# Layer 0's first gate: its sums moved from matmuls to weighed sums, and its product with the heads moved to the fourth head

## The chip, the cores and the metric

The kernel runs on one core of a Trainium2 chip. The time is the device time of one execution in microseconds (us). The core has five engines that run side by side, each through its own list of instructions: TensorE (PE, matrix products), VectorE (DVE), ScalarE (ACT), GpSimd (POOL), and SyncE (SP), which issues most of the transfers from HBM. On-chip data lies in SBUF (128 partitions); PE writes its results into PSUM, eight banks of 128x512 fp32.

## The reference

A transformer of two layers on 256 latent tokens `x` and 256 context tokens `ctx`, width 1024, in fp32. Each layer makes six vectors from a condition (`c` for the latents, `c_ctx` for the context), and uses them as shift, scale and gate around a mixer and an MLP:

```python
mod = (silu_c @ ada_w[i] + ada_b[i])[:, None, :]
mod_c = silu_cc @ ada_w[i] + ada_b[i]
sh1, sc1, g1, sh2, sc2, g2 = jnp.split(mod, 6, axis=-1)
h = x * (1.0 + sc1) + sh1
y, yc = retention_mixer(h, hc, ...)          # layer 0; layer 1: neighbourhood_mixer
x = layer_norm(DN_ALPHA * x + g1 * y, ln_g[i, 0], ln_b[i, 0])
h = x * (1.0 + sc2) + sh2
x = layer_norm(DN_ALPHA * x + g2 * sq_relu_mlp(h, mlp_w1[i], mlp_w2[i]), ln_g[i, 1], ln_b[i, 1])
```

In layer 0 the context takes the same way with `sh1c`, `g1c` and so on. The retention mixer has four heads; the result of each, `o`, is normalized, multiplied by `silu(gate projection)`, and goes through its 512 rows of `w_o`; `y` is the sum over the four heads. So `g1 * y` is a product of a vector over the 1024 columns with the sum of four heads' outputs.

## The kernel before

**Numbers and weights.** Each fp32 product is made of three matmuls (`mm3`) on parts: a high part, cast to a shorter format, and a low part, the difference. Weights come in units of 128x1024 (512 KB). A unit is loaded on SP's queue into a raw slot (`fetch`, L255; the pool `rawp` has four slots), ACT casts it (`hi`), DVE subtracts (`lo`), and PE uses both. `hi` and `lo` have five buffers each, so that up to five units are prepared ahead (`take`, L282). A raw slot is free again when `lo` is made.

**The order.** Each helper records every operation through one line, L84, so all rows carry that line, and one goes by the names of the tiles. A scheduler fixes each engine's order when the kernel is built; places where `dve.on` or `act.on` is set keep the order of the code. On the chip each engine goes through its list in order, and an instruction that waits holds up all behind it on its engine, also on the queues of SP and POOL.

**Tiles.** The residual `R` has four tiles of 128 tokens by 1024: 0 and 1 (latents) lie in one buffer, `R_104`, and 2 and 3 (context) in another, `R_105`. At first they hold x and ctx.

**The heads** (`for h in range(RH)`, L1045). The first head's q and v are made in a prologue. Then for each head: `pq` (q, then k, two units each), rotation by position (`rotate`, L1003: ACT casts, DVE products and sums), `pv` (four units) and its evacuation into `vh` by ACT and `vl` by DVE, the scores `pS` (24 matmuls) masked by DVE, the gate projections `pg` of tiles 0 and 1, `po` (scores by v), the other two gate projections, a transposition, and the output products `pw` of the head's 512 rows of `w_o`. The first head has the order `pg` (tile 0), `pS`, `pg` (tile 1), `po`. For each `pw` piece of 128x512, `accumulate` (L756) multiplies by the gate `G` on DVE and adds the result to R on POOL. So R must hold `ALPHA * x` before: two ACT operations of 128x2048 in the first head scale it. In the fourth head both go to DVE, since the layer norm waits for them.

**The condition's sums ("ada").** `ada_w` has 6144 columns for each layer, and their products with `silu(c)` are made little by little beside the main work, in parts named (layer, 0 mixer or 1 MLP, 0 and 1 for shift and scale, 2 for gate). A generator, `bg_stream` (L535), yields after each step; `bg()` (L605) is called at fixed places of the code and advances it by a step, up to a bound `bg_max` (39 in the heads, then 87 in the MLP). A step uses one unit of 512 KB that takes a raw slot too (`rawa`). There are two forms:

- The first gate, part (0, 0, 2), is made on PE (`ada_mm`, L440): matmuls with the condition as the stationary side into the bank `pada`, its bias is loaded (`ada_bias`), DVE adds the two (`ada_row`), and the row goes to DRAM (`grow`) and comes back spread over all partitions as `G` (`load_gate`, L616), by POOL's queue. It fills the first nine steps, in the first head.
- All other parts are *weighed* (`weigh`, L521): DVE multiplies a raw unit by one number per partition and adds it to a sum. In layer 0's heads the sums are four 128x512 operations a step, into `strips` that nothing else uses then; later they are 128x1024 (`acc`). After the last step the sum is folded: DVE reduces it to `red`, and PE adds over the partitions with one small product (`pada`), in `ada_columns` or, for a gate, `ada_gate` (L488).

In the heads, 14 steps come in the first, 10 in the second and third each, and 5 in the fourth. The MLP (`hf` loop, L1312) has two halves of eight `p` products (two units each, 10.9 us on PE) and two output products of eight units.

## Time and profile before

| | us |
|---|---|
| median of three runs | 1186.15 (1185.89 to 1186.85) |
| the profiled execution | 1188.31 |
| its span, first to last instruction | 1186.5 |
| PE busy in the span | 1176.7 |
| DVE / ACT / POOL busy | 832.8 / 480.9 / 248.9 |
| granted clock of PE, mean | 0.999 |

All durations and places in time below are from the one profiled execution; its time is 2.16 us above the median. A row of the chain of waits or of a timeline gives the start in the span, the duration, the engine, the tile that is written (for timelines also what is read and the shape), and how many instructions the row holds. In brackets stands the idle time of that engine ahead of the row and what ended it.

### The profile page before, as it was taken

The page shows a single profiled execution, that of the slowest core. Times are in us where ns is not written, and L with a number is a line of the kernel's source. Part 1 is how long each engine was busy: PE and PEld are TensorE (multiplying, and loading weights), DVE is VectorE, ACT ScalarE, POOL GpSimd, SP SyncE. Part 2 cuts the span into 40 slices and gives each one's busy share as a digit, 9 for nine tenths or more (in the row PEclk, how much of TensorE's full clock was granted, in tenths as well). Part 3 has the DMA queues.
Part 4 walks back from the last instruction along what each step waited for, and adds up shares of the span by engine and source line. Part 5 has one row for each costly group of instructions (what it writes and reads, how often), then busy time and mean ns, then how long its engine had stood idle before and what let it go on. Part 6 is the DMA issues. An engine that isn't in the chain of part 4 may idle for free.

```text
span 1186.5 us, 17867 instructions
## 1 busy us (share of the span) xinstructions
PE 1176.7 (99%) x6884; PEld 990.9 (84%) x6884; DVE 832.8 (70%) x1304; ACT 480.9 (41%) x813; POOL 248.9 (21%) x389
## 2 busy tenths in 40 slices
PE   9999999999999999999999999999999999999997
PEld 7778888888888889888888888889888878999886
DVE  3876975886688487757876675668467588876446
ACT  3652222322223246441212333137466666665341
POOL 0104301310330141780202000223344430000001
PEclk9999999999999999999999999999999999999999
DMA  9964441444254216756566665637244434765660
GB/s 276 273 234 161 142 158 56 143 130 137 89 160 160 77 55 209 203 112 215 177 193 211 200 213 185 206 108 215 69 143 125 118 122 152 224 201 185 227 212 36
DMA packets 138041, 193.16 MB, mean 163 GB/s; under 512 B 9772, under 2 KB 81108, under 8 KB 137956
## 3 DMA queue, kind: packets, MB, share of 16 engines
q1 hardware_dynamic: 129572, 179.02, 47.3%
q0 software_dynamic: 7232, 10.44, 3.9%
q10 hardware_dynamic: 1152, 2.56, 0.7%
q8 instruction: 54, 0.88, 0.3%
q14 instruction: 31, 0.25, 0.1%
HBM read 187.15 MB, written 5.75 MB: 163 GB/s over the span
## 4 chain that ended last, share of the span: by engine, by line
PE 96%; ACT 1%; DVE 1%; issue 1%; DMA 0%; POOL 0%; DVEq 0%; ACTq 0%
PE p L84 44%; PE pq L84 8%; PE pg L84 7%; PE pv L84 7%; PE pw L84 7%; PE pn L84 5%; PE pnv L84 4%; PE po L84 3%; PE pada L84 2%; PE pnw L84 1%; PE pS L84 1%; PE ppt L84 1%; PE pqk L84 1%; PE pt L84 1%; PE pav L84 1%; PE p1t L84 1%
## 5 line engine op out<-in xcount | busy, mean ns | idle before, releaser
L84 ACT CAST hi<-raw 128x1024 fp32r<-128x1024 f32 (+2 forms) x228 | 232.7, 1032 | 325.0 <-PE p L84 151.3
L84 DVE TENSOR_TENSOR lo<-raw,hi 128x1024 fp32r<-128x1024 f32 (+2 forms) x228 | 280.3, 1240 | 101.8 <-ACT hi L84 101.0
L84 PE MATMUL p<-hi,hid 128*128 128x512 f32 (+1 forms) x832 | 241.8, 374 | 0.0
L84 PEld LDWEIGHTS p<-hi,hid 128*128 128x128 f32 x832 | 152.1, 188 | 27.7
L84 PE MATMUL p<-hTh,lo 128*128 128x256 f32 (+1 forms) x512 | 166.9, 329 | 0.0
L84 PE MATMUL p<-hTl,hi 128*128 128x256 f32 (+1 forms) x512 | 166.9, 329 | 0.0
L84 PE MATMUL p<-hTh,hi 128*128 128x256 f32 (+1 forms) x512 | 164.0, 330 | 0.0
L84 PE MATMUL p<-lo,hid 128*128 128x512 f32 (+1 forms) x416 | 155.3, 373 | 0.0
L84 DVE SCALAR_TENSOR_TENSOR acc<-rawa,scol,acc 128x1024 f32<-128x1024 f32 x56 | 74.7, 1344 | 63.1 <-DMA rawa<-in_ada_w_dram 62.9
L84 POOL TENSOR_TENSOR R<-R,acc 128x512 f32<-128x512 f32 x40 | 62.2, 1565 | 212.3 <-DVE acc L84 212.2
L84 PEld LDWEIGHTS p<-hTl,hi 128*128 128x128 f32 x512 | 96.4, 188 | 8.7
L84 PEld LDWEIGHTS p<-hTh,lo 128*128 128x128 f32 x512 | 96.3, 188 | 8.8
L84 PEld LDWEIGHTS p<-hTh,hi 128*128 128x128 f32 x512 | 95.1, 190 | 8.7
L84 PEld LDWEIGHTS p<-lo,hid 128*128 128x128 f32 x416 | 78.4, 188 | 13.6
L84 ACT CAST hid<-r 128x256 fp32r<-128x256 f32 (+1 forms) x64 | 31.9, 500 | 103.4 <-DVE r L84 103.3
L84 DVE SCALAR_TENSOR_TENSOR strips<-rawa,scol,strips 128x512 f32<-128x512 f32 x84 | 66.4, 847 | 0.0
L84 POOL TENSOR_TENSOR rstd<-rstd,misc 128x1 f32<-128x1 f32 x28 | 19.2, 686 | 215.5 <-DVE rstd L84 214.3
L84 ACT ACTIVATE s<-s,mn 128x512 f32<-128x512 f32 x64 | 45.5, 712 | 26.2 <-DVE mn L84 26.1
L84 PE MATMUL pg<-hi,hTh 128*128 128x512 f32 x128 | 51.1, 399 | 0.0
L84 PE MATMUL pw<-hi,oh 128*128 128x512 f32 x128 | 50.9, 398 | 0.0
L84 PE MATMUL pg<-lo,hTh 128*128 128x512 f32 x128 | 50.0, 391 | 0.0
L84 PE MATMUL pw<-hi,ol 128*128 128x512 f32 x128 | 50.0, 390 | 0.0
(238 smaller groups left out, 2277.1 us busy)
## 6 DMA issues: line engine op xcount, KB each, us to landing
raw<-in_mlp_w_dram SPq DMA_DIRECT2D x128, 512.0 KB, 4.2
rawa<-in_ada_w_dram SPq DMA_DIRECT2D x80, 512.0 KB, 4.3
raw<-in_ret_w_in_dram SPq DMA_DIRECT2D x42, 512.0 KB, 3.6
raw<-in_nat_w_in_dram SPq DMA_DIRECT2D x24, 512.0 KB, 3.9
rawq<-in_ada_w_dram SPq DMA_DIRECT2D x16, 512.0 KB, 5.8
raw<-in_ret_w_o_dram SPq DMA_DIRECT2D x16, 512.0 KB, 4.4
bias<-rpb_rows POOLq DMA_DIRECT2D x32, 128.0 KB, 2.9
raw<-in_nat_w_o_dram SPq DMA_DIRECT2D x8, 512.0 KB, 4.1
```

The lines of the kernel that those rows point to most:

```text
L84: r = f(*args, **kwargs)
```

## The change

The first gate becomes a weighed sum like the next two parts (these three are now called `EARLY`), and its matmuls, bias load and row addition on DVE go. The MLP's gate, part (0, 1, 2), which was weighed in the heads, moves into the first half of the MLP, as two 128x1024 operations a step; so the heads have as many weighed steps as before (24), with bounds 31 and 88 for the stream. The first head has 6 steps now, the others 9, 10 and 6.

Since the gate is there later, the first three heads' outputs are added without it. In the first head ACT copies `pw` into R; in the second and third DVE adds `pw` to R. The gate is loaded on SP's queue at the start of the third head. In the fourth, `residual_in` does for each of the four tiles what is left: the tile of x or ctx is loaded once more, into a raw slot (`rawx`), POOL multiplies R by the gate, ACT scales `rawx` by ALPHA, and POOL adds it to R. The fourth head's own output is gated as before. The load of the MLP's gate (`G2`) is issued four units later, and the second half of the MLP takes up to three steps in each `p` product.

```diff
-    def ada_bias(l, offs, nb):
...
-    def ada_mm(pr, k, nb, rhs):
...
-    def ada_row(pr, brow, nb, p0=0, p1=P, row=None):
...
-    def on_pe(l, w, part):
-        return (l, w, part) == (0, 0, 2)
+    EARLY = (0, 0, 2), (0, 1, 0), (0, 1, 1)
-        if l == 1 or w == 0:
+        if (l, w, part) not in EARLY:
...
         for l, w, part in (
-            [(0, 0, 2), (0, 1, 0), (0, 1, 1), (0, 1, 2)]
-            + [(1, 0, 0), (1, 0, 1), (1, 0, 2), (1, 1, 0), (1, 1, 1), (1, 1, 2)]
+            list(EARLY)
+            + [(0, 1, 2), (1, 0, 0), (1, 0, 1), (1, 0, 2), (1, 1, 0), (1, 1, 1), (1, 1, 2)]
         ):
             sh, sc, g = 3 * w * D, (3 * w + 1) * D, (3 * w + 2) * D
             offs = (sh + 512 * part, sc + 512 * part) if part < 2 else (g, g + 512)
             for n in range(KC):
                 plan.append((l, w, part, offs, n))
-        nxt = bg_load(*plan[0])
-        yield
+        nxt = None
         for step, (l, w, part, offs, n) in enumerate(plan):
-            raw = nxt
-            if step + 1 < len(plan):
+            if nxt is None:
+                nxt = bg_load(l, w, part, offs, n)
+                yield
+            raw, nxt = nxt, None
+            if step + 1 < len(plan) and step + 1 != len(EARLY) * KC:
                 nxt = bg_load(*plan[step + 1])
             nt = 2 if l == 0 or (w == 0 and part < 2) else 1
-            if on_pe(l, w, part):
-                if n == 0:
-                    pr = bank("pada")
-                if n == KC - 2:
-                    brow = ada_bias(l, offs, 256)
-                ada_mm(pr, n, 256, lambda j: raw[:, j // 2, (j % 2) * 256 : (j % 2 + 1) * 256])
-                if n == KC - 1:
-                    row = ada_row(pr, brow, 256)
-                    for t in range(2):
-                        pool.dma_start(
-                            out=grow[l, w][t].rearrange("(j c) -> j c", j=4), in_=row[t:P:32, :]
-                        )
-                yield
-                continue
             if n == 0:
                 red = smp.tile([P, 2, 32], F32, tag="red", name=nm("red"), bufs=2)
-            if l == 0:
+            if (l, w, part) in EARLY:
                 dve.on = True
                 for kk in range(2):
                     for t in range(nt):
...
-                    dve.on = n == 0 and (w, part) == (0, 0)
+                    dve.on = n == 0 and l == 0
...
-    bg_max = [39]
+    bg_max = [31]
...
-            if first:
-                bg(2)
...
             act.copy(out=vh[:, t, :], in_=pv[t][:])
             dve.tensor_sub(out=vl[:, t, :], in0=pv[t][:], in1=vh[:, t, :].bitcast(F32))
-    G1s = [None]
-
-    def first_gate():
-
-        if G1s[0] is None and bg_done[0] >= 9:
-            G1s[0] = load_gate(0, 0, eng=nc.gpsimd)
+    def residual_in(t):
+
+        raw = rawp.tile([P, D], F32, tag="raw", name=nm("rawx"))
+        sp.dma_start(out=raw[:], in_=(x, ctx_in)[t // 2][0][tsl(t % 2), :])
+        pool.tensor_mul(out=R[t], in0=R[t], in1=G1[:, t // 2, :])
+        act.mul(out=raw[:], in_=raw[:], mul=ALPHA)
+        pool.tensor_add(out=R[t], in0=R[t], in1=raw[:])
     for h in range(RH):
         last = h == RH - 1
-            act.on = True
-            for a in range(2):
-                act.mul(out=RR[a][:], in_=RR[a][:], mul=ALPHA)
-            act.on = False
-            proj_T(qkh[:, 2:4], qkl[:, 2:4], True)
+            proj_T(qkh[:, 2:4], qkl[:, 2:4])
         else:
             qkh = slot(S_TH, [P, 4, NT], F32R, "qkh")
             qkl = slot(S_TL, [P, 4, NT], F32R, "qkl")
+            if h == 2:
+                G1 = load_gate(0, 0, eng=nc.sync)
+            if last:
+                residual_in(0)
             proj_T(qkh[:, 0:2], qkl[:, 0:2])
+            if last:
+                residual_in(1)
             proj_T(qkh[:, 2:4], qkl[:, 2:4])
             vh = slot(S_VH, [P, 4, DV], F32R, "vh")
             vl = slot(S_VL, [P, 4, DV], F32R, "vl")
...
+                if last and u % 2 == 0:
+                    residual_in(2 + u // 2)
                 bg()
             evac_v(pv, vh, vl)
         qh, ql, kh, kl = qkh[:, 0:2], qkl[:, 0:2], qkh[:, 2:4], qkl[:, 2:4]
...
-                if h == 0 and k == 3 and len(ts) == 1:
-                    bg(2)
-                    first_gate()
...
-                bg()
+                if (h, t) != (1, 1):
+                    bg()
...
         def tok(t, half, us):
-            accumulate(tok_mm(t, half, us), t, half, G1)
+            ps = tok_mm(t, half, us)
+            o = R[t][:, half * 512 : (half + 1) * 512]
+            if h == 0:
+                act.copy(out=o, in_=ps[:])
+            else:
+                dve.tensor_add(out=o, in0=ps[:], in1=o)
         if not last:
             for half in range(2):
...
-            bg_until(39)
+            bg_until(31)
...
-        bg_max[0] = 87
+        bg_max[0] = 88
...
-                bg(2 + fp % 2)
+                bg(3 if fp > 1 else 2)
+            elif fp > 4:
+                bg(3 if fp > 5 else 1)
             if hf == 0 and fp < 6:
                 for q in range(16 * (fp - 2), 16 * (fp - 1)):
                     shifted_biases(q)
-        if G2 is None:
-            G2 = load_gate(0, 1)
         for half in range(2):
             last = hf == 1 and half == 1
             pb = [bank("p2") for _ in range(4)]
...
                 bg()
+                if G2 is None and u == 3:
+                    G2 = load_gate(0, 1)
             if not last:
                 for t in range(4):
                     accumulate(pb[t], t, half, G2)
                 continue
-            bg_until(87)
+            bg_until(88)
             held = take(4)
```

How the instructions stand, at three places. First PE in the first head, at the end of the gate's first product and the start of the scores. In the names, `hi` and `lo` are parts of weights, `hTh` and `hTl` of the modulated input, `qkh` and `qkl` of q and k. Before:

```order
L84 MATMUL pg_900<-hi_835,hTh 128x512
L84 MATMUL pada_828<-rawa_913,cT 32x256 x4
L84 MATMUL pg_900<-lo_836,hTh 128x512
L84 MATMUL pg_900<-hi_835,hTl 128x512
L84 MATMUL pS_940<-qkh_760 128x256
L84 MATMUL pS_940<-qkl_761,qkh_760 128x256
L84 MATMUL pS_940<-qkh_760,qkl_761 128x256
```

After:

```order
L84 MATMUL pg_877<-hi_824,hTh 128x512
L84 MATMUL pg_877<-lo_825,hTh 128x512
L84 MATMUL pg_877<-hi_824,hTl 128x512
L84 MATMUL pS_905<-qkh_760 128x256
L84 MATMUL pS_905<-qkl_761,qkh_760 128x256
L84 MATMUL pS_905<-qkh_760,qkl_761 128x256
L84 MATMUL pS_916<-qkh_760 128x256
```

The matmuls into `pada` (`rawa` is the raw unit, `cT` the condition) no longer stand between those of the gate, and the second score bank follows the first after three matmuls. Next, POOL between the third head's last gate products (`gs`) and the fourth head's first normalization (`rstd`). Before:

```order
L84 TENSOR_TENSOR gs_2509<-sg_2774,gs_2509 128x512
L84 TENSOR_TENSOR R_104<-R_104,acc_2814 128x512
L84 TENSOR_TENSOR R_104<-R_104,acc_2837 128x512
L84 TENSOR_TENSOR R_105<-R_105,acc_2866 128x512
L84 TENSOR_TENSOR R_105<-R_105,acc_2882 128x512
L84 TENSOR_TENSOR R_104<-R_104,acc_2916 128x512
L84 TENSOR_TENSOR R_104<-R_104,acc_2932 128x512
L84 TENSOR_TENSOR R_105<-R_105,acc_2954 128x512
L84 TENSOR_TENSOR R_105<-R_105,acc_2970 128x512
L84 TENSOR_SCALAR rstd_3425<-mv_3423 128x1
```

After (`G_2092` is the gate, `rawx` the loaded tiles of x and ctx):

```order
L84 TENSOR_TENSOR gs_2415<-sg_2673,gs_2415 128x512
L84 TENSOR_TENSOR R_104<-R_104,G_2092 128x1024 x2
L84 TENSOR_TENSOR R_105<-R_105,G_2092 128x1024
L84 TENSOR_TENSOR R_104<-R_104,rawx_2871 128x1024
L84 TENSOR_TENSOR R_105<-R_105,G_2092 128x1024
L84 TENSOR_TENSOR R_104<-R_104,rawx_2962 128x1024
L84 TENSOR_TENSOR R_105<-R_105,rawx_3083 128x1024
L84 TENSOR_TENSOR R_105<-R_105,rawx_3156 128x1024
L84 TENSOR_SCALAR rstd_3339<-mv_3337 128x1
```

Eight additions of 128x512 become four products and four additions of 128x1024. Third, SP's queue in the fourth head, from the load of k's second unit (`128x4x256`) on. Before:

```order
L84 DMA raw_2979<-in_ret_w_in_dram 128x4x256
L84 DMA raw_2985<-in_ret_w_in_dram 128x2x512
L84 DMA raw_3015<-in_ret_w_in_dram 128x2x512
L84 DMA raw_3065<-in_ret_w_in_dram 128x2x512
L84 DMA raw_3095<-in_ret_w_in_dram 128x2x512
L84 DMA raw_3149<-in_ret_w_in_dram 128x2x512
L84 DMA rawa_3179<-in_ada_w_dram 128x2x512
L84 DMA raw_3185<-in_ret_w_in_dram 128x2x512
L84 DMA rawa_3215<-in_ada_w_dram 128x2x512
L84 DMA raw_3221<-in_ret_w_in_dram 128x2x512
L84 DMA rawa_3251<-in_ada_w_dram 128x2x512
L84 DMA raw_3257<-in_ret_w_in_dram 128x2x512
```

After:

```order
L84 DMA raw_2878<-in_ret_w_in_dram 128x4x256
L84 DMA raw_2884<-in_ret_w_in_dram 128x2x512
L84 DMA raw_2914<-in_ret_w_in_dram 128x2x512
L84 DMA rawx_2962<-in_x_dram 128x1024
L84 DMA raw_2969<-in_ret_w_in_dram 128x2x512
L84 DMA raw_2999<-in_ret_w_in_dram 128x2x512
L84 DMA raw_3053<-in_ret_w_in_dram 128x2x512
L84 DMA rawx_3083<-in_ctx_dram 128x1024
L84 DMA raw_3090<-in_ret_w_in_dram 128x2x512
L84 DMA rawa_3120<-in_ada_w_dram 128x2x512
L84 DMA raw_3126<-in_ret_w_in_dram 128x2x512
L84 DMA rawx_3156<-in_ctx_dram 128x1024
```

Two of the four loads of `rawx` stand here between the weights, the third at the end, and the first just ahead. By the waits that the build gives, `raw_2884` (v's first unit) takes the slot of the first, `rawx_2871`, and waits for the POOL addition that reads it; `raw_3053` (the first of the gate) takes that of `rawx_2962`, and `rawa_3120` that of `rawx_3083`. And DVE at the end of the fourth head's `pv`, after:

```order
L84 SCALAR_TENSOR_TENSOR strips_119<-rawa_3120,scol,strips_119 128x512
L84 TENSOR_TENSOR lo_3170<-raw_3167,hi_3169 128x1024
L84 SCALAR_TENSOR_TENSOR strips_118<-rawa_3161,scol,strips_118 128x512
L84 SCALAR_TENSOR_TENSOR strips_119<-rawa_3161,scol,strips_119 128x512
L84 SCALAR_TENSOR_TENSOR strips_118<-rawa_3161,scol,strips_118 128x512
L84 SCALAR_TENSOR_TENSOR strips_119<-rawa_3161,scol,strips_119 128x512
L84 TENSOR_TENSOR vl_3048<-pv_3049,vh_3047 128x512
L84 TENSOR_TENSOR vl_3048<-pv_3050,vh_3047 128x512
```

The first `vl`, which frees the first of the four `pv` banks, stands behind the weighings of `rawa_3161` and the subtraction of the unit ahead of them, as it stood before behind those of `rawa_3251`.

30 lines of the change are left out of this document (1 added, 29 removed).

## The prediction

> **What bounds the kernel now.** I read the page's busy times first, then the chain that ended last, then the timelines of the engines where the chain and the change meet.
>
> ```profile
> PE 1176.7 (99%) x6884; PEld 990.9 (84%) x6884; DVE 832.8 (70%) x1304; ACT 480.9 (41%) x813; POOL 248.9 (21%) x389
> ```
>
> TensorE (PE) is busy for 99% of the span, 1176.7 of 1186.5 us; no other engine passes 70%. So time is won only by PE rows that vanish, and lost only where PE starts to wait. The chain in the first head, where the removed sums stand (`pada`; `pq`, `pg`, `pS` are the projection, gate and score products):
>
> ```profile
> 60.14 5.50 PE pq L84 x24
> 65.64 0.57 PE pada L84 x8
> ...
> 71.88 1.00 PE pada L84 x16
> 72.88 2.99 PE pg L84 x12
> ...
> 80.16 4.18 PE pS L84 x24
> ...
> 91.85 8.16 PE po L84 x36
> ```
>
> Each row begins where the one ahead of it ends (60.14 + 5.50 = 65.64, 71.88 + 1.00 = 72.88; the left-out rows too), so PE is in one piece from 60.14 to 91.85, 31.71 us. What the same products take where no `pada` stands between them is seen in the later heads, and the second fence has the fourth head, where the gate and the residual are put in:
>
> ```profile
> 134.54 21.76 PE pq L84 x96
> 182.25 10.88 PE pg L84 x48
> ...
> 337.93 21.76 PE pq L84 x96
> 359.69 21.76 PE pv L84 x96
> 381.45 4.18 PE pS L84 x24
> 385.63 10.88 PE pg L84 x48
> ```
>
> **The part that goes.** The stretch holds 48 `pq`, 48 `pg` and 24 `pS`. At 21.76/96 and 10.88/48, both 0.2267 us each, and 4.18 for the scores, they need 10.88 + 10.88 + 4.18 = 25.94 us. The rest, 31.71 - 25.94 = 5.77 us, is what the removed rows cost PE: 0.57 or 1.00 for each group, and what the products just behind run longer (2.99 instead of 2.72 for 12). The removed bias loads, the row add on DVE and the gate's stores stood beside this and are worth nothing; neither are the two scalings of R on ACT, since no ACT row is on the chain here.
>
> **What is added on PE.** The gate is now folded like the other parts, by one `pada` product of 32x64 in the tail of the second head. Its price is that of such a fold in the fourth head's tail:
>
> ```profile
> 416.48 0.23 PE pada L84 x2
> 416.71 2.96 PE pw L84 x12
> ```
>
> 0.23 for two, plus 2.96 - 2.72 = 0.24 for the twelve products behind them: 0.47 us at most. Net on PE: 5.77 - 0.47 = 5.30 us less. With this alone the profiled run of 1188.31 us becomes 1183.0; the runs' median is 1186.15, 2.16 below it, and would become 1180.85. All times below stand against the median.
>
> **First three heads.** ACT copies (first) or DVE adds straight from PSUM (second, third) in place of DVE products and POOL adds; ACT was no bound (41%). DVE still has one 512-wide instruction a piece, and the POOL adds go; nothing waited there on the chain, so I take 0. One exposed place: the first head's scores follow the gate's first product with less PE work ahead, so the rotation of k has less cover. The scores now take all first-half parts first, 2.5 us of the 4.18; between 0 and 0.7 us, I take 0. The gate load is issued on SP at the start of the third head, a head ahead of its use. The bias loads that SP loses, and the store and load of the gate that POOL's queue loses, were not waited for.
>
> **The fourth head.** Here the change adds four loads of x or ctx (512 KB each) on SP's queue, each in one of the four raw slots through which all weights go, four scalings on ACT, and eight POOL instructions of 128x1024: R times gate, then R plus scaled x, for each of four tiles. POOL's order is multiply, multiply, multiply, add 0, multiply, adds 1 to 3. The slots matter: the load of v's first weights now waits for add 0; the first gate weights wait for add 1, and two background loads for adds 2 and 3. Rows for POOL's price, 512 wide, and DVE's beside it:
>
> ```profile
> 319.62 1.29 POOL L84 TENSOR_TENSOR R<-R,acc 128x512 f32<-128x512 f32 x1 [1.76 <-DVE acc L84]
> 329.49 1.73 POOL L84 TENSOR_TENSOR R<-R,acc 128x512 f32<-128x512 f32 x1 [1.76 <-DVE acc L84]
> 342.25 2.21 POOL L84 TENSOR_TENSOR R<-R,acc 128x512 f32<-128x512 f32 x1 [0.49 <-DVE acc L84]
> 329.34 3.76 DVE L84 SCALAR_TENSOR_TENSOR strips<-rawa,scol,strips 128x512 f32<-128x512 f32 x4
> 367.71 2.73 DVE L84 SCALAR_TENSOR_TENSOR strips<-rawa,scol,strips 128x512 f32<-128x512 f32 x4
> ```
>
> Alone a POOL add takes 1.29 us; beside weighings on DVE (329.34) 1.73; 2.21 at 342.25, beside weight subtractions. The DVE group suffers too: 3.76 us against 2.73 with POOL idle. The Trainium skill, "SBUF — State Buffer", section "Who interferes with whom", says that a DVE instruction with two SBUF inputs and a POOL instruction that reads SBUF lock each other out for a whole instruction; the rows agree, and by that rule a POOL add that lets one subtraction of 1.22 us pass would take 2.58 + 1.22 = 3.80 us at double width; with that in the sum below, the time would be 1184.4.
>
> At double width: 2.58, 3.46 or 4.42 us. The first can start at about 333.1: R's first two tiles share a buffer, and are whole when the sixth of the third head's eight output products (they end at 337.93, 2.72 apart: the sixth at 332.5) has been added, 0.6 by `vl`'s row below. Add 0, the fourth, then ends at 343.3, 346.8 or 350.7.
>
> What hangs on it, in the order of the queues, is one chain: v's first weights land, are cast and split; the third of v take a slot behind them; x's third load a slot behind those; ACT, in order, scales that one before it casts k for its rotation; DVE, in order, rotates k and only then splits the gate's weights, weighs, and last evacuates v (`vl`). The first gate product needs the PSUM bank that `vl` frees. Prices:
>
> ```profile
> 365.21 1.05 ACT L84 CAST hi<-raw 128x1024 fp32r<-128x1024 f32 x1 [0.57 <-PE pv L84]
> 366.57 1.22 DVE L84 TENSOR_TENSOR lo<-raw,hi 128x1024 fp32r<-128x1024 f32 x1
> 357.01 0.37 ACT L84 CAST qkh<-pq 128x256 fp32r<-128x256 f32 x1 [1.85 <-PE pq L84]
> 357.48 1.29 DVE L84 TENSOR_TENSOR t<-pq,cst 128x256 f32<-128x256 f32 x3 [1.07 <-ACT qkh L84]
> 358.81 0.42 DVE L84 TENSOR_TENSOR qkl<-pq,qkh 128x256 fp32r<-128x256 f32 x1
> 359.15 0.42 DVE L84 TENSOR_TENSOR t<-t 128x256 f32<-128x256 f32 x1
> 359.60 0.41 ACT L84 CAST qkh<-t 128x256 fp32r<-128x256 f32 x1 [2.22 <-DVE t L84]
> 380.97 2.48 DVE L84 TENSOR_TENSOR vl<-pv,vh 128x512 fp32r<-128x512 f32 x4
> ```
>
> and, from the DMA view of the same stretch, the landings (the last number, in us):
>
> ```profile
> raw<-in_ret_w_in_dram SPq DMA_DIRECT2D x10, 512.0 KB, 3.6
> raw<-in_ret_w_o_dram SPq DMA_DIRECT2D x4, 512.0 KB, 4.3
> ```
>
> Two times landing 3.6, cast 1.05, split 1.22: 11.7. Landing and scaling of x: 4.65. Rotation of k's first half 0.37 + 2.13 + 0.41 = 2.9; cast and split 2.3; second half 2.5; cast and split 2.3; weighing 2.7 (367.71); split 1.2; landing, cast, split of the last gate weights 5.9; weighing 2.7; first `vl` 0.6. Sum 39.5 us. `vl` then ends at 382.8, 386.3 or 390.2, and the first `pg` wants its bank at 385.63 (it was free at 381.6 before). PE waits 0, 0.7 or 4.6 us. If the chain's four landings take 4.3 us, as the ret_w_o loads did, instead of 3.6, it is 2.8 more: 0, 3.5 or 7.4. So the bounds are 0 and 7.4. I take 346.8, since 1.73 is the price beside weighings, which DVE does then too, and landings halfway, as the queue carries 2 MB more in that stretch: 0.7 + 1.4 = 2.1 us. After that wait PE has scores and gates ahead of it, and the masked scores are ready before `po` asks for them; the fold on POOL in the tail replaces DMA issues there: 0.
>
> **The MLP.** The MLP gate's sums leave the heads for the first half of the MLP: two 128x1024 weighings a step, three steps in each of the seventh and eighth products, and faster pace later.
>
> ```profile
> 542.64 2.48 DVE L84 SCALAR_TENSOR_TENSOR acc<-rawa,scol,acc 128x1024 f32<-128x1024 f32 x2 [0.20 <-DMA rawa<-in_ada_w_dram]
> ```
>
> The same engine over those two products (the window, PE, PE's weight loads, DVE, ACT, POOL):
>
> ```profile
> 509.00:531.00 22.00, 22.00 (x99) 18.21 (x98) 12.76 (x15) 8.88 (x12) 19.95 (x35) 1.00 0.55 116
> ```
>
> Those two products' 22 us have DVE busy for 12.76 us; six steps of 2.48 add 14.9, 5.6 us more than the stretch has. The cover is the lead of split weights, five buffers of 5.44 us of PE work; a shortfall of 5.6 fits in four units' lead, 21.8 us, unless landings come late too. POOL's 19.95 us there are DMA issues (x35, no tensor operation), so I count no lock on the weighings. The G2 load goes after the fourth unit of the second product, half a product before its use. I take 0, bounds 0 and 3.
>
> **Sum.** -5.77 + 0.47 + 2.1 = -3.2: 1183.0 us from the median.
>
> **Rivals.** *Hidden* (chance 0.20): POOL's block ends by 344 or the slots come round in another way, and PE waits under 0.8 us: 1180.8 to 1181.7. For it: DVE is busy for only 40.41 of the 48 us before `pg`, by the window below, so 7.6 us of lateness could be made up.
>
> ```profile
> 338.00:386.00 48.00, 48.00 (x219) 39.99 (x218) 40.41 (x65) 15.29 (x24) 3.50 (x2) 1.00 0.49 156
> ```
>
> Against: the chain's idle time lies in landings that DVE can't hasten, and POOL never had four double-width instructions in a row beside DVE.
>
> *Given back* (0.15): POOL at 2.21 a half, slow landings: a wait of 4.7 to 7.4, 1185.5 to 1188.3, no measurable change. For it is the row at 342.25; against it that this row is the slowest of POOL's in this stretch.
>
> *Slower* (0.25): the same wait grows long enough that PE restarts at its cold pace. How a cold start goes is seen at the beginning:
>
> ```profile
> 1.23 3.78 PE pq L84 x16
> PEclk9999999999999999999999999999999999999999
> ```
>
> Sixteen products of 256 columns take 0.236 us each, where in `pS` (9216 columns in 4.18 us) 256 columns take 0.116: 1.9 us lost on that row; the clock's line, in slices of 30 us, doesn't resolve it. A wait of 5.8 us with 1.9 behind it is 7.7, 2.4 more than the 5.30 gained, and from there the kernel is slower: 1188.5, up to 1192 with DVE's shortfall in the MLP on top. For it: every delay in the fourth head adds on one chain of five in-order steps, with only 2.8 us to spare if POOL is undisturbed. Against: before's trace has no PE wait in this stretch. The Trainium skill, "TensorE: Matmul & The Clock Gate", section "Part 1: The HAM clock gate", puts the throttle's window at about 3.4 us of idleness; no trace here shows PE idle that long, and by it the loss would begin already at a wait of 3.4 us.
>
> **Chances and range.** The forecast, a wait of 0.8 to 4.7 us (1181.7 to 1185.5), has 0.40. 0.2%, 2.4 us, is about what measurement tells from no change. Faster than 1183.8: all of "hidden" and a little over half of the forecast, 0.42. Slower than 1188.5: 0.25. Between: 0.33. The range from 1181.1 to 1189.6 leaves out about 0.08 below and 0.11 above.
>
> **What would show it.** Right: no `pada` between 60 and 92 us, and `po` of the first head about 5.8 us earlier; eight 128x1024 POOL rows between the third and fourth heads, the first ones at 3 to 4 us; the first `pg` of the fourth head waiting for `vl` by 1 to 4 us. Wrong: PE idle elsewhere (the first head's scores, the seventh and eighth products of the MLP, G2), POOL rows near 2.6 us and no wait (faster), or a row of slow products behind a long wait (slower).

## The result and the profile after

| | median, us | range | runs |
|---|---|---|---|
| before | 1186.15 | 1185.89 to 1190.5 | 5 |
| after | 1196.71 | 1194.12 to 1199.03 | 5 |

The ratio is 1.0081, with a 95% interval of 1.0057 to 1.0104: the kernel became 0.8% slower, by 10.6 us. The profiled execution took 1197.7 us with a span of 1195.9, against 1188.31 and 1186.5: 9.4 us more in the span, which the rows below account for. In the experiments further down, medians and ratios leave out one slow execution each of x_nores (4132.57 us) and x_mlp0 (1659.6 us).

```profile
PE 1174.1 (98%) x6822; PEld 990.2 (83%) x6822; DVE 846.0 (71%) x1315; ACT 484.0 (40%) x823; POOL 233.1 (19%) x372
```

TensorE (PE) is busy for 2.6 us less than before, in a span that is 9.4 us longer: the removed work is gone, and waits have come. The chain of the first head:

```profile
59.91 10.94 PE pq L84 x48
70.86 5.44 PE pg L84 x24
76.30 4.20 PE pS L84 x24
80.49 5.44 PE pg L84 x24
85.94 8.16 PE po L84 x36
```

No `pada` stands there, and `po` starts at 85.94 instead of 91.85: 5.91 us earlier. That lead is still there at the fourth head's scores. Then the whole of it goes. PE's waits, summed over the execution (engine and tile, what it waited for, us, times, longest):

```profile
PE pg L84 <- DVE vl L84: 5.9, 1, 5.9
PE pada L84 <- DVE red L84: 3.3, 2, 1.8
PE p L84 <- DVE lo L84: 2.1, 3, 1.4
```

None of these three is in the trace of before. The chain from the fourth head's gate on, and the same places before:

```profile
385.64 14.00 PE pg L84 x48
399.64 8.16 PE po L84 x36
444.87 2.87 PE p L84 x24
808.93 2.87 PE pn L84 x24
```

```profile
441.76 2.87 PE p L84 x24
797.23 2.87 PE pn L84 x24
```

The gate products wait 5.9 us and then take 14.00 us, where 48 of them took 10.88 before. The reader sees why in the timeline: the durations of single matmuls behind the wait, and the granted clock (third number from the end) of the 14 us.

```profile
386.24 0.63 PE L84 MATMUL pg<-lo,hTh 128*128 128x512 f32 x1
391.77 0.39 PE L84 MATMUL pg<-hi,hTl 128*128 128x512 f32 x1
386.00:400.00 14.00, 14.00 (x51) 11.31 (x51) 10.20 (x18) 3.32 (x7) 0.00 (x0) 0.80 0.38 118
```

So the account, in the one profiled execution: -5.9 in the first head; +5.9 of waiting and +3.1 of slow clock in the fourth, which puts the MLP's first product (`p`, 444.87) 3.1 us behind; +8.6 in layer 0's MLP, which takes 364.1 us from `p` to layer 1's first product (`pn`, 808.93) instead of 355.5. That makes +11.7, of which +9.4 is left at the end of the span. The last MLP wins back 2.8 us of it, with the same instructions, first before, then after:

```profile
1016.92 162.12 PE p L84 x1104
1028.33 159.34 PE p L84 x1104
```

These 2.8 us don't come from the change: the same row takes 162.12 us in the profiles of x_nores, x_mlp0, x_pool, f_a2, f_af and f_lim below, and 159.33 in those of x_both, x_dma, f_fold and f_thin. What decides between the two values is not known. So a difference of this size between the times of two profiled executions is no evidence by itself, and medians can carry a part of it; the places of the rows up to layer 1 are free of it.

The MLP's 8.6 us: two folds wait for DVE's reduction, 3.3; behind the second one the clock is slow again, about 1.7; waits for split weights, 2.1; one fold more in the MLP, about half a us by the prediction's price for one; the rest is spread.

```profile
598.62 0.26 PE L84 MATMUL pada<-red,cst 128*32 128x16 f32 x8 [1.76 <-DVE red L84]
600.16 1.06 PE L84 MATMUL p<-hi,hid 128*128 128x512 f32 x2
604.43 0.62 PE L84 MATMUL p<-hi,hid 128*128 128x512 f32 x2
```

After a wait of 1.76 us, pairs of matmuls take 1.06 us from 600 to 603, and then 0.62.

What the chain consists of in the MLP (430 to 812 us) shows where the waits come from. First before, then after; `rawa` are the loads of the condition's units, `acc` their weighings:

```profile
by line: PE p L84 91.9%; PE pn L84 3.4%; PE pw L84 2.9%; PE pt L84 1.6%; PE pada L84 0.3%
by line: DMA rawa<-in_ada_w_dram 32.1%; PE p L84 25.7%; DVE acc L84 13.7%; issue 7.9%; DVE lo L84 6.7%; DMA raw<-in_mlp_w_dram 4.6%; PE pw L84 3.4%; PE pt L84 1.5%; DVE hid L84 0.9%; PE pn L84 0.8%; DVE red L84 0.7%; DVE r L84 0.7%; ACT hi 
```

Before, only PE stands there. After, 32.1% of the stretch are landings of `rawa`: DVE, in order, waits for such a load ahead of a weighing, and the splitting of the MLP's weights (`lo`) stands behind it.

### The profile page after: what moved, and what is told of

Its sections match the earlier page's. It is cut to its first block, busy times and chain, and to the rows that moved or that the text cites. A ratio compares the mean times of both kernels' runs of the same rounds, so it can differ in the third digit from the quotient of the medians.

```text
span 1195.9 us, 17719 instructions
## 1 busy us (share of the span) xinstructions
PE 1174.1 (98%) x6822; PEld 990.2 (83%) x6822; DVE 846.0 (71%) x1315; ACT 484.0 (40%) x823; POOL 233.1 (19%) x372
## 3 DMA queue, kind: packets, MB, share of 16 engines
q10 hardware_dynamic: 1152, 2.56, 0.7%
## 4 chain that ended last, share of the span: by engine, by line
PE 69%; DMA 13%; DVE 11%; issue 4%; ACT 3%; DVEq 0%; POOL 0%; ACTq 0%
PE p L84 22%; DMA rawa<-in_ada_w_dram 10%; PE pg L84 8%; PE pw L84 6%; PE pq L84 6%; PE pv L84 6%; PE pn L84 5%; DVE acc L84 4%; PE pnv L84 4%; DVE lo L84 3%; PE po L84 3%; DVE strips L84 2%; DMA raw<-in_mlp_w_dram 1%; PE pnw L84 1%; PE ppt L84 1%
## 5 line engine op out<-in xcount | busy, mean ns | idle before, releaser
L84 DVE TENSOR_TENSOR lo<-raw,hi 128x1024 fp32r<-128x1024 f32 (+2 forms) x228 | 274.9, 1218 | 107.6 <-ACT hi L84 107.3
L84 DVE SCALAR_TENSOR_TENSOR acc<-rawa,scol,acc 128x1024 f32<-128x1024 f32 x70 | 90.1, 1308 | 53.4 <-DMA rawa<-in_ada_w_dram 53.1
L84 POOL TENSOR_TENSOR R<-R,acc 128x512 f32<-128x512 f32 x16 | 24.8, 1569 | 145.8 <-DVE acc L84 145.8
L84 DVE TENSOR_TENSOR hid<-r,hid 128x256 fp32r<-128x256 f32 (+1 forms) x64 | 34.5, 540 | 26.5 <-ACT hid L84 26.4
L84 PE MATMUL pg<-hi,hTl 128*128 128x512 f32 x128 | 50.9, 398 | 0.0
```

What stands on the lines that cost most here:

```text
L84: r = f(*args, **kwargs)
```

## The experiments

Two theories stand after the result. *A*: the fourth head and the MLP lose separately, each for a cause of its own. *B*: the fourth head hands its queues over late, and the MLP's loss follows. Within the fourth head, *L*: POOL's operations lock out DVE's weighings; *S*: the loads of x and ctx take raw slots and time in SP's queue. All times are medians, and each ratio is against the kernel before, run beside it on the same chip (there its median was 1186.9 to 1188.1).

| run | us | ratio, 95% interval | layer 0's MLP, us |
|---|---|---|---|
| x_nores | 1190.85 | 1.0025 (1.0009 to 1.0041) | 362.7 |
| x_mlp0 | 1195.51 | 1.0066 (1.0047 to 1.0085) | 358.4 |
| x_both | 1186.22 | 0.9982 (0.9969 to 0.9994) | 361.9 |
| x_pool | 1199.95 | 1.0110 (1.0077 to 1.0142) | 364.4 |
| x_dma | 1189.14 | 1.0016 (1.0003 to 1.0028) | 363.8 |
| f_a2 | 1192.18 | 1.0036 (1.0015 to 1.0056) | 364.5 |
| f_fold | 1205.99 | 1.0156 (1.0140 to 1.0173) | 373.9 |
| f_af | 1199.64 | 1.0102 (1.0087 to 1.0118) | 373.3 |
| f_thin | 1189.58 | 1.0016 (1.0004 to 1.0028) | 365.7 |
| f_v2 | 1184.43 | 0.9980 (0.9970 to 0.9989) | 355.5 |
| f_v3 | 1181.21 | 0.9951 (0.9936 to 0.9965) | 355.5 |
| f_lim | 1180.82 | 0.9942 (0.9928 to 0.9957) | 355.5 |

The last column is from the first `p x24` row of the chain to layer 1's first `pn x24`, in each run's profile: 355.5 before, 364.1 after.

**Without residual_in.**

```diff
     def residual_in(t):
-        raw = rawp.tile([P, D], F32, tag="raw", name=nm("rawx"))
-        sp.dma_start(out=raw[:], in_=(x, ctx_in)[t // 2][0][tsl(t % 2), :])
-        pool.tensor_mul(out=R[t], in0=R[t], in1=G1[:, t // 2, :])
-        act.mul(out=raw[:], in_=raw[:], mul=ALPHA)
-        pool.tensor_add(out=R[t], in0=R[t], in1=raw[:])
+        return
```

> The changed kernel with the whole of residual_in left out: no load of x and ctx, no product of R with the gate, no scaling, no addition (so layer 0's residual and the gate of the first three heads are missing from the result); the MLP as in the changed kernel. Theory A, two separate losses (fourth head 5.9 us of waiting for vl and 3.1 us at the slow clock behind it; MLP about 8.6 us): 9.0 us less than the changed kernel's 1196.7, about 1187.7, no wait for vl, the two waits of the MLP's folds still there. Rival B, the MLP runs late only because the fourth head handed its queues over late: about 1180 to 1182, and no waits in the MLP.

```profile
436.37 2.87 PE p L84 x24
799.07 2.87 PE pn L84 x24
```

The wait for `vl` is gone, and the MLP begins 8.5 us earlier than after, though this execution came 0.6 us later out of the prologue (`pv x8` at 58.56 instead of 58.00). So by the places of the rows the fourth head's 9 us are won back in full. The MLP still took 362.7 us, with one of the two waits for folds left, 2.0 us: rival B falls, since the MLP is slow though the fourth head is on time. The median fell by only 5.9 us, to 1190.85, and lies above what A and B expected. In the profile, 2.8 us of what the fourth head won are lost again in the last MLP, which took its longer value, 162.12.

**Without the MLP gate's sums, pace of before.**

```diff
-            + [(0, 1, 2), (1, 0, 0), (1, 0, 1), (1, 0, 2), (1, 1, 0), (1, 1, 1), (1, 1, 2)]
+            + [(1, 0, 0), (1, 0, 1), (1, 0, 2), (1, 1, 0), (1, 1, 1), (1, 1, 2)]
...
-                bg(3 if fp > 1 else 2)
-            elif fp > 4:
-                bg(3 if fp > 5 else 1)
+                bg(2 + fp % 2)
```

> The changed kernel without the sums of the MLP gate (part (0, 1, 2) is left out; the first gate is loaded in its place), and the background steps of the MLP at the pace of the kernel before; the fourth head as in the changed kernel. Theory A: 8.6 us less than 1196.7, about 1188.1, with the wait for vl of 5.9 us still there. Rival B: the wait in the fourth head makes the MLP late, so the MLP loses its 8 us here too and the time stays at 1194 to 1196.

```profile
PE pg L84 <- DVE vl L84: 6.4, 1, 6.4
PE p L84 <- DVE lo L84: 2.1, 2, 1.6
```

The MLP's folds no longer wait, and it takes 358.4 us, 5.7 less than after. The median fell by only 1.2 us, and the two ratios, 1.0066 and 1.0081, can't be told apart. In the profile, 1.3 us of the 5.7 went ahead of the first head (`pv x8` at 59.28 instead of 58.00) and 2.8 in the last MLP (162.12). The time lies where B expected it, but not for B's reason: the fourth head waited 6.4 us, and the MLP lost 2.9 and not 8.6. So most of the MLP's loss comes with the added steps and their pace, and not all.

**Both.** The two edits above together.

> Both left out: residual_in and the MLP gate's sums (the residual, the gate of three heads and the MLP's own gate are missing from the result), the MLP at the pace of before. What is left of the change is the first head without the sums on TensorE, and the added fold. Theory A and rival B: 1186.15 - 5.9 + 0.5, about 1180.7. If a third loss hides in the first three heads (ACT copies, DVE additions): more than that, 1183 or above.

1186.2 and not 1180.7, where before had 1187.9 on this chip. The loss is not in the first three heads, which the expectation named for such a time: the MLP begins at 436.07, 5.7 us ahead of before. It lies in the MLP, which takes 361.9 us, 6.4 more than before, with both suspects gone. Its one large wait is near its end:

```profile
PE p L84 <- DVE lo L84: 3.3, 3, 2.5
```

2.5 us of these stand at 775 us, with about 1.8 us of slow clock behind them. The MLP here has 49 background steps at the pace at which before has 48, since the change no longer loads ahead over the border between heads and MLP; the last one falls behind the last call. That this one step is the cause was argued from the place, and not tried alone. The versions at the end have 49 steps too, but begin them earlier, at an even pace, and have no such wait (355.5 us); so the number of steps alone doesn't decide.

**POOL's operations alone.**

```diff
-        raw = rawp.tile([P, D], F32, tag="raw", name=nm("rawx"))
-        sp.dma_start(out=raw[:], in_=(x, ctx_in)[t // 2][0][tsl(t % 2), :])
         pool.tensor_mul(out=R[t], in0=R[t], in1=G1[:, t // 2, :])
-        act.mul(out=raw[:], in_=raw[:], mul=ALPHA)
-        pool.tensor_add(out=R[t], in0=R[t], in1=raw[:])
+        pool.tensor_add(out=R[t], in0=R[t], in1=G1[:, t // 2, :])
```

> The changed kernel with residual_in cut to its two POOL operations a tile: R times the gate, then R plus the gate in place of x (so the residual is wrong); no load, no raw slot, no scaling on ACT. The MLP as in the changed kernel. Theory L (POOL's operations lock out DVE's weighings, and that alone makes vl late): the four weighings beside POOL still take 6 to 9 us instead of 2.7, the wait for vl stays above 3.4 us and the slow clock with it, 1193 to 1197. Theory S (the raw slots and the loads of x in the queue make vl late): no wait for vl, like the kernel without residual_in, about 1187.7. Both halves needed: a wait of 1 to 3 us, 1189 to 1191.

**The loads alone.**

```diff
-        pool.tensor_mul(out=R[t], in0=R[t], in1=G1[:, t // 2, :])
         act.mul(out=raw[:], in_=raw[:], mul=ALPHA)
-        pool.tensor_add(out=R[t], in0=R[t], in1=raw[:])
```

> The changed kernel with residual_in cut to its other half: the four loads of x and ctx into raw slots and ACT's scaling of them, and no POOL operation (the gate of three heads and the residual are missing from the result). The MLP as in the changed kernel. Theory L (POOL locks out DVE): no wait for vl, or under 1 us, and the time of the kernel without residual_in, 1191.2, within 1 us. Theory S (slots and landings alone suffice too): a wait for vl of 3 us or more, and 1194 to 1197.

These two bear on L and S. POOL and DVE at the end of the third head, first in the changed kernel:

```profile
322.67 2.73 DVE L84 SCALAR_TENSOR_TENSOR strips<-rawa,scol,strips 128x512 f32<-128x512 f32 x4
327.65 6.65 DVE L84 SCALAR_TENSOR_TENSOR strips<-rawa,scol,strips 128x512 f32<-128x512 f32 x4
335.42 8.77 DVE L84 SCALAR_TENSOR_TENSOR strips<-rawa,scol,strips 128x512 f32<-128x512 f32 x4
327.22 5.21 POOL L84 TENSOR_TENSOR R<-R,G 128x1024 f32<-128x1024 f32 x2 [15.71 <-DVE R L84]
334.98 2.39 POOL L84 TENSOR_TENSOR R<-R,G 128x1024 f32<-128x1024 f32 x1 [2.56 <-DVE R L84]
337.33 2.86 POOL L84 TENSOR_TENSOR R<-R,rawx 128x1024 f32<-128x1024 f32 x1
340.15 2.84 POOL L84 TENSOR_TENSOR R<-R,G 128x1024 f32<-128x1024 f32 x1
```

with POOL's operations alone (the last row is from PE's waits):

```profile
328.02 10.91 DVE L84 SCALAR_TENSOR_TENSOR strips<-rawa,scol,strips 128x512 f32<-128x512 f32 x4
341.18 10.70 DVE L84 SCALAR_TENSOR_TENSOR strips<-rawa,scol,strips 128x512 f32<-128x512 f32 x4
327.58 10.80 POOL L84 TENSOR_TENSOR R<-R,G 128x1024 f32<-128x1024 f32 x4 [15.74 <-DVE R L84]
PE pg L84 <- DVE vl L84: 5.9, 1, 5.9
```

and with the loads alone:

```profile
332.04 2.74 DVE L84 SCALAR_TENSOR_TENSOR strips<-rawa,scol,strips 128x512 f32<-128x512 f32 x4
337.04 2.73 DVE L84 SCALAR_TENSOR_TENSOR strips<-rawa,scol,strips 128x512 f32<-128x512 f32 x4
```

Four weighings take 2.73 us without POOL, and 10.91 where four POOL operations (10.80 us) stand beside them: each weighing waits out one whole operation of POOL. The changed kernel fits the same price: beside two operations 2 x 2.6 + 2 x 0.68 = 6.6 us (6.65 measured), beside three 3 x 2.7 + 0.68 = 8.8 (8.77). With all eight POOL operations there, the wait for `vl` is 5.9 us with no load at all, and the median lies above the range that L gave; but those eight hold up the weighings more than the five of the changed kernel do there (21.6 us for eight weighings instead of 15.4), so the equal waits don't show an equal cause. With the loads and no POOL operation there is no wait, and the time is 7.6 us less than after. So without POOL's operations there is no loss in the fourth head, and S alone does nothing; whether the five would do it without the loads, these two don't show. The Trainium skill, "SBUF — State Buffer", section "Who interferes with whom", says that a DVE instruction with two SBUF inputs contends with a POOL instruction that reads SBUF, that the shared pair of ports is an exclusive lock, and that the order of issue decides who blocks. 10.91 against 10.80 us for four and four agrees with the lock.

**The fourth head mended.**

```diff
-            if h == 2:
-                G1 = load_gate(0, 0, eng=nc.sync)
-            if last:
-                residual_in(0)
...
-            if last:
-                residual_in(1)
...
-                if last and u % 2 == 0:
-                    residual_in(2 + u // 2)
+                if last and u == 2:
+                    G1 = load_gate(0, 0, eng=nc.sync)
...
             S = masked_scores()
             for t in range(2):
+                if last:
+                    residual_in(2 * t)
+                    residual_in(2 * t + 1)
                 pg = gate(t)
```

> The changed kernel with the gate loaded in the middle of the fourth head's v product, and residual_in called behind the scores, so that the same eight POOL operations and four loads run while DVE works from PSUM (masks, statistics). The whole computation is there. Theory L: the weighings of the third head's end are back at 2.7 us for four, no wait for vl, about 1191 like the kernel without residual_in. Rival: POOL's block now delays the first normalization (rstd) of the fourth head, and the PE waits for it ahead of the transposes by 2 to 5 us: 1193 to 1196.

The later call of the gate's load changed nothing in SP's list, so the four products stayed where they were; the loads, scalings and additions moved behind the scores.

```profile
327.95 6.63 DVE L84 SCALAR_TENSOR_TENSOR strips<-rawa,scol,strips 128x512 f32<-128x512 f32 x4
336.85 6.42 DVE L84 SCALAR_TENSOR_TENSOR strips<-rawa,scol,strips 128x512 f32<-128x512 f32 x4
379.38 5.36 POOL L84 TENSOR_TENSOR R<-R,rawx 128x1024 f32<-128x1024 f32 x2 [37.99 <-ACT rawx L84]
387.38 5.35 POOL L84 TENSOR_TENSOR R<-R,rawx 128x1024 f32<-128x1024 f32 x2 [2.64 <-ACT rawx L84]
380.01 10.88 PE pg L84 x48
```

The weighings didn't come back to 2.7 us as L expected: they are still locked out by the products. And yet PE doesn't wait: `pg` begins at 380.01, 5.6 us ahead of before, in 10.88 us, and the first `rstd` stands at 396.04 instead of 400.27. So the 7.6 us by which DVE is held up there are made up, when v's weights aren't behind loads of x as well. The wait of the changed kernel needs more than the four products: either the additions in the same block (as with POOL alone), or the loads between the weights. Which of the two is not shown; in the changed kernel's chain, the third load of x and ctx alone, from issue to landing, is 5.78 us. The MLP still takes 364.5 us, and the time is 4 us above before.

**The folds later.**

```diff
     def flush(done=None):
-        while due:
-            due.pop(0)()
+        while due and (done is None or due[0][0] <= done):
+            due.pop(0)[1]()
...
+                due.append((bg_done[0] + (0 if (l, w, part) in EARLY else 2), fn))
...
-                if G2 is None and u == 3:
+                if G2 is None and u == 6:
```

> The changed kernel with the folds of the parts that are weighed in the MLP put two background steps later in TensorE's list (some 11 us), and the MLP gate's load three units later; nothing else. Theory F (TensorE waits in the MLP because a fold stands in its list ahead of DVE's reduction, and then runs at the slow clock): the two waits for red (3.3 us) and about 1.5 us of slow clock go, 1191.9. Rival D (DVE and the raw slots are late as a whole, and the wait comes back as one for split weights, lo, further on): 1195 to 1197, with more than 2.1 us of waiting for lo.

**Both moves.**

> Both moves together, the whole computation there: residual_in behind the fourth head's scores, and the folds of the MLP two steps later. If theories L and F hold and the losses are separate: 1196.7 - 9.0 - 4.8, about 1183, below the kernel before by 3. If the stream of loads and weighings of the MLP is the bound once TensorE no longer waits in the fourth head, as the kernel with both parts left out suggests (its MLP took 361.9 us against 355.5 before): 1186 to 1189.

```profile
PE p L84 <- DVE mod L84: 6.8, 1, 6.8
PE p L84 <- DVE lo L84: 6.3, 5, 2.1
```

Theory F, that the MLP loses by the place of its folds, falls as a remedy. The waits for the reduction went, but `p` waited 6.8 us for `mod`, the reading of a fold's result from its PSUM bank, which DVE now did late while the MLP's products needed the bank; and the waits for `lo` grew from 2.1 to 6.3, as rival D has it, though D's 1195 to 1197 had no place for `mod`. With both moves the MLP was as slow (373.3), with 7.2 us for `mod`.

**Loads without DVE's work.** The fourth head mended as above, and the MLP gate's weighings after its first step cut to 8 columns, its loads as they are:

```diff
-                    weigh(acc[:, t], raw[:].rearrange("p a n -> p (a n)"), t, n, n == 0)
+                    nc_ = 8 if (l, w, part) == (0, 1, 2) and n > 0 else D
+                    weigh(acc[:, t][:, :nc_], raw[:].rearrange("p a n -> p (a n)")[:, :nc_], t, n, n == 0)
```

> The changed kernel with the fourth head mended (gate loaded late, residual_in behind the scores), and the MLP gate's weighings after the first step cut to 8 of 1024 columns, so that its loads, raw slots, fold and gate load all stay and some 17 us of DVE work in the MLP go (the MLP's gate is wrong). That mended kernel's MLP took 364.5 us from the first p product to the first product of layer 1, against 355.5 in the kernel before. Theory D (DVE's time is what the MLP lacks): 356 to 358, and a total near 1184. Theory Q (the eight more loads through the four raw slots are what it lacks): 362 to 365, and a total near 1190, with the waits for lo still above 3 us.

```profile
PE p L84 <- DVE lo L84: 6.6, 5, 2.0
by line: DMA rawa<-in_ada_w_dram 36.2%; PE p L84 25.7%; DVE acc L84 10.1%; issue 7.4%; DVE lo L84 6.6%; DMA raw<-in_mlp_w_dram 5.0%; PE pn L84 2.3%; PE pt L84 1.5%; PE pw L84 1.4%; DVE red L84 1.0%; ACT hi L84 0.8%; DVE r L84 0.5%; DVE hid 
```

365.7 us, as slow as with the weighings, and 6.6 us of waits for `lo`. DVE's time for the weighings is not what the MLP lacks, and the landings of `rawa` are 36.2% of the chain from 430 to 812 us here. So theory Q is what is left: the added loads, in one queue and four slots with the weights, at the pace at which they are asked for. The loads were not taken out alone, with the fold and the pace kept.

**The last gate in the last MLP.** The fourth head mended as above, and:

```diff
-            + [(0, 1, 2), (1, 0, 0), (1, 0, 1), (1, 0, 2), (1, 1, 0), (1, 1, 1), (1, 1, 2)]
+            + [(0, 1, 2), (1, 0, 0), (1, 0, 1), (1, 0, 2), (1, 1, 0), (1, 1, 1)]
...
-                bg(3 if fp > 1 else 2)
+                bg(2)
...
-                bg(3 if fp > 5 else 1)
+                bg(2 if fp > 5 else 1)
...
-                if G2 is None and u == 3:
+                if G2 is None and u == 6:
...
-    G2 = load_gate(1, 1, 1)
+    def late_stream():
+        acc = [scr("late") for _ in range(2)]
+        red = smp.tile([P, 2, 32], F32, tag="red", name=nm("red"), bufs=2)
+        nxt = ada_load(1, 0, (5 * D, 5 * D + 512))
+        yield
+        for n in range(KC):
+            raw = nxt
+            if n + 1 < KC:
+                nxt = ada_load(1, n + 1, (5 * D, 5 * D + 512))
+            for i in range(2):
+                weigh(acc[i][:], raw[:, i, :], 0, n, n == 0)
+            yield
...
+        ada_gate(1, 1, red, 1)
+        yield
+
+    late = late_stream()
...
+            if f4 > 2:
+                next(late, None)
...
     for u in range(13):
+        next(late, None)
+        if u == 5:
+            G2 = load_gate(1, 1, 1)
```

> The whole computation: the fourth head mended as before (gate loaded late, residual_in behind the scores); the last part of the sums, the gate of layer 1's MLP, taken out of layer 0's MLP and weighed in layer 1's MLP, where it is used; so layer 0's MLP has 49 background steps, as the kernel before had 48, at two a product in its second half. If the MLP's loss is the number of steps in it (by theory D or Q): its time 356 to 358, the total 1181 to 1184, if layer 1's MLP hides eight loads and sixteen 512-wide weighings, as its DVE is busy for half its time. Rival: layer 1's MLP, which takes a weight unit every 2.7 us, waits for weights, and the gain is lost there: 1186 to 1190.

```profile
435.88 2.87 PE p L84 x24
791.39 2.87 PE pn L84 x24
PE p L84 <- DVE lo L84: 2.2, 3, 0.8
by line: PE p L84 91.9%; PE pn L84 4.9%; PE pt L84 1.5%; PE pw L84 1.4%; PE pada L84 0.3%
```

The MLP of layer 0 takes 355.51 us, as before (355.47), with the MLP gate's sums in it and no wait, and no landing stands in its chain any more (the last row, 430 to 812 us). The three short waits are in layer 1's MLP.

**The same, three products later.**

```diff
-            if f4 > 2:
+            if f4 > 5:
                 next(late, None)
...
-        if u == 5:
+        if u == 8:
             G2 = load_gate(1, 1, 1)
```

> The whole computation: the version with the last gate in layer 1's MLP, its steps started three products later there, so that most of them fall into the second matrix's part, where DVE has no activation to do. If the three waits for lo (2.2 us) between 1056 and 1081 us came from DVE's and ACT's order in the first matrix's part: they go, 1182 to 1183. If they come from the loads through the raw slots, which take one unit every 2.7 us there too: they move along, and the time stays at 1184 to 1185.

The waits are gone, so they came from the place of the steps beside the first matrix and not from the loads as such: 1181.21 us (1180.93 to 1183.46), 0.9951 of the kernel before. This version computes the whole and is faster than both kernels: by 0.5% than before, and, by the two ratios, by 1.3% than after.

**The limit.** The last gate's sums left out (`(1, 1, 2)` out of the plan, no `late_stream`).

> The same version with the last gate's sums left out altogether (layer 1's mixer gate is loaded in its place, so the result is wrong): the limit of what the move off TensorE can give. With no wait left but those of the kernel before: 5.9 us less on TensorE, 0.5 for the added fold and its group, so 5.4 below the kernel before, 1181.5 where that has 1186.9. If it stays within 2 us of the kernel before, a loss is hidden that the waits don't show.

1180.82, within 0.4 us of the version that does the sums. Its profile has the last MLP at 162.12 us like that of before, and a span of 1181.0 instead of 1186.5: 5.5 us less, where 5.4 were expected (the medians on this chip differ by 7.3). So what the move off TensorE can give is all but reached by the version above, and no loss is hidden in the first heads.

## Why the prediction was wrong

The prediction was 1183.0 in a range of 1181.1 to 1189.6, with 0.25 for slower; measured were 1196.7. Three terms of its sum were too small: the wait in the fourth head (2.1, measured 5.9), the slow clock behind it (nothing, 3.1) and the MLP (nothing, 8.6). With the first two alone, -5.9 + 5.9 + 3.1 = +3.1, the sum would be 1189.3, inside the range; the MLP takes it outside.

- *The part that goes* held: 5.77 us forecast, 5.91 measured.
- *What is added on PE*, 0.47 in the second head's tail, isn't seen in the heads: they had three folds before and have three now, since the MLP gate's went to the MLP. The 5.9 us are whole up to the fourth head.
- *First three heads*: 0 forecast, 0 measured, the first head's scores too (4.20 us against 4.18).
- *The fourth head* was mis-sized: 2.1 us of waiting forecast within 0 to 7.4, 5.9 measured. The chain of the working (v's weights, x's third load, k's rotation, gate weights, `vl`) is the one the profile shows. Its start, the end of add 0, came where it was forecast: 346.8 on the clock of before is 340.9 with the lead of 5.9, and it was 340.2. That was luck: POOL took 2.4 to 2.9 us an operation and not 3.46, but paused for 2.56 us between. The step that failed is the length of the chain behind it, 45.4 us instead of 39.5 and 1.4 for slow landings. From the end of add 0 to the split of v's first unit it took 7.5 us, and from there to that of the third 7.5, where the working had 5.9 each; x's third load with its scaling took 7.0 instead of 4.65; the rest 23.5 instead of 23.1. A part of this is the lock, which the working priced on POOL while DVE paid: eight weighings took 15.4 us instead of 5.5, until 344.2, and held up the split of v's first unit.
- *The slower rival's mechanism*, a wait and then a cold PE, is what happened there: 5.9 and 3.1 us, where it had 5.8 and 1.9. The price of the slow clock was too low, and it came in the MLP too, after a wait of 1.76 us, which the rival didn't have. It ended higher than the rival's 1192, since the rival gave the MLP at most 3 us.
- *The MLP* is the step that cost most: "I take 0, bounds 0 and 3"; measured 8.6 us. The working weighed DVE's 5.6 us of shortfall against the lead of split weights, and took a stream of loads for free. The runs showed that DVE's time for the weighings is not the point (365.7 us with most of it gone), that the number and the pace of the added steps are (355.5 us with eight steps fewer at two a product), with landings of their loads on the chain (32.1% of the stretch, none before), and that a fold in PE's list is a wait by itself when DVE is late.
- Of what was named as a sign of being wrong, "PE idle elsewhere ... the seventh and eighth products of the MLP, G2" pointed at the right stage, though the waits lie in the products after those.

What stays open: whether the five POOL operations of the changed kernel would make PE wait without the loads of x and ctx; what loads, fold and pace each cost in the MLP, and the single added step at its end; and why the last MLP takes one of two values.

## What to carry to other kernels

When PE is busy for 99% of the span, moving work from it to engines that are "70% busy" is worth what PE loses, but only where the work finds room in the queue that carries it: count loads, slots and the place of each fold in PE's list, stage by stage, and not the other engine's share. A block of POOL operations that read SBUF cost DVE here one whole POOL operation for each weighing beside it (10.91 us for four instead of 2.73), so put such a block where nothing that PE needs soon stands behind DVE's work on SBUF. Behind the fourth head's scores (f_a2) it still held up four weighings (7.02 us), and PE didn't wait. A wait of PE may not be paid for when it ends: look for slow matmuls behind it.

## What the runs showed of the hardware

The clock fell after shorter waits than expected. Here a wait of 5.9 us was followed by 6 us of matmuls at 0.63 instead of 0.39 us (0.43 apart instead of 0.23), and a wait of 1.76 us by some 3 us of them (the rows at 600.16). The length of the wait doesn't decide alone: behind waits of 1.87 us (f_af, at 688), 2.00 (x_nores, 549), 2.47 (x_both, 775) and 2.58 (x_pool, 557) the matmuls were slow too, and behind waits of 1.55 (after, 557), 1.90 (x_nores, 776), 2.04 (f_thin, 779) and 2.14 (f_fold, 660) they were not. The rows behind the wait in f_thin:

```profile
779.18 0.50 PE L84 MATMUL p<-lo,hid 128*128 128x512 f32 x1 [2.04 <-DVE lo L84]
779.52 0.62 PE L84 MATMUL p<-hi,hid 128*128 128x512 f32 x2
780.21 0.62 PE L84 MATMUL p<-hi,hid 128*128 128x512 f32 x2
```

The Trainium skill, "TensorE: Matmul & The Clock Gate", section "Part 1: The HAM clock gate", gives a window of about 3.4 us that runs freely. That waits of about the same length came out both ways agrees with a window that runs freely, though no run here shows the window itself. Waits well below 3.4 us can cost the clock too: there the measurement decides.

Which side pays for the lock was unexpected: POOL's 128x1024 operations hardly slowed down (2.4 to 2.9 us, one 3.57), while DVE's 128x512 weighings went from 0.68 to 1.7, 2.2 and 2.7 us each, as means of four.
